# Moving where the split weights begin in their tiles: 52 bytes instead of 64

## The chip, the cores and the metric

The kernel runs on one core of a Trainium2 chip. The metric is the device time of one execution in microseconds; the shown number is the median of three executions.

## The reference, cut to what matters

Two transformer blocks run one after the other on 256 tokens of width 1024. The first has a gated feed-forward layer (width 2816), a mixer with two kinds of attention and gates, and a second gated feed-forward layer. The second has a mixer of a convolution and a retention, a cross attention to 256 memory rows, and a feed-forward layer of width 4096 with a squared ReLU. Everything is float32. Nearly all the work is in products of activations with weight matrices that are read once:

```python
def swiglu(h, w_in, w_out):
    gu = h @ w_in
    gate, up = jnp.split(gu, 2, axis=-1)
    return (jax.nn.silu(gate) * up) @ w_out
...
def sq_relu_mlp(h, up_w, down_w):
    return jnp.square(jax.nn.relu(h @ up_w)) @ down_w
```

## The kernel before, in words

**Layout.** Activations lie feature by token: 128 features of a block on the partitions, the tokens along the free dimension (272 tokens up to the first attention, because of 16 meta tokens; 256 from there on). A weight block of 128 by 128 is the stationary operand of a matmul and the activations are the moving operand. `_plan` (L43) writes down the order in which all weight blocks are used and packs them into chunks of up to 2048 columns.

**Three products for one.** Each factor is split into a high part in the chip's reduced float32 format (fp32r) and a low part, the rest. `mm3` (L512) makes three matmuls for each weight block: high weight by high activation (L513), high weight by low activation (L514), low weight by high activation (L515). Each of them loads its weight block anew. Counting the loops of the program there are 2,360 blocks that go this way, so 7,080 such matmuls, and 144 more in `products_t` (L995), where the weight part is the moving operand (512 columns, L1005 to L1007) and the activation is loaded.

**The split of the weights.** `_Weights` brings a chunk into a tile `raw` by DMA (`load`, L291), ScalarE writes the high part (`_high`, L319) and VectorE the low part (`piece`, L335). `piece` is called between the other work in `_Core.step`, so that the parts are ready ahead of their use. The tiles `hi` and `lo` come from `_part`, three of each: a tile is 64 columns (`LINE`) wider than the chunk, and the part begins `SHIFT` columns behind the tile's start:

```python
        t = self.pool.tile([P, CH + LINE], F32R, tag=tag, bufs=3, name=f"{tag}{c}")
        return t[:, SHIFT : SHIFT + CH]
```

**Where operands begin.** The tiles that serve as moving operands of `mm3` (`XH`, `XL`, `AH`, `AL`, `YH`, `YL`, `MH`, `ML`, `CH`, `CL` and the like) and their rows per block are multiples of 64 columns, that is of 256 bytes, and so are the `hi` and `lo` tiles. All of them therefore begin at one place modulo 256 bytes. A weight block has 128 columns (512 bytes), so each block begins as many bytes behind that place as the whole part does: 64 with `SHIFT` 16. Some matmuls take their moving operand in two pieces of 128 columns, the second 576 bytes behind the first (`qv`, L498); the call is `xq`. In one product (`fa`) the weight blocks are only 8 columns wide, so that successive blocks begin 32 bytes apart.

**Other matmuls.** Scores, transposes, statistics (`rms`, L559, matmul L562) and head norms (L766) run in plain float32; they break the stream of the fp32r matmuls at the borders of the layers and all through the attention.

Of the kernel before, what the change touches and what calls it, by code (L numbers as in the profile page):

```python
# [23 lines left out]
TP = 288  # L24
XP = 320
LINE = 64
SHIFT = 16
DFF = 2816
MF = DFF // P
DFF2 = 4096  # L30
# [244 lines left out]
class _Weights:  # L275
# [30 lines left out]
    def _part(self, tag, c):  # L306


        t = self.pool.tile([P, CH + LINE], F32R, tag=tag, bufs=3, name=f"{tag}{c}")
        return t[:, SHIFT : SHIFT + CH]  # L310

# [1294 lines left out]
```

## Time and profile before

| what | value |
|---|---|
| median of 3 executions | 982.52 us |
| lowest, highest | 981.97, 982.52 us |
| the profiled execution's own time | 983.64 us |
| its span, first to last instruction | 981.6 us |
| mean granted TensorE clock | 0.998 |
| TensorE: matmuls, busy share | 7,667, 98% |
| VectorE, ScalarE busy share | 69%, 55% |

The profile is of one execution. Of its 983.64 us, 981.6 lie between the first and the last instruction and some 2 around them. A matmul's record runs from its start until its result is out, so the records of successive matmuls overlap; the time that one takes from the next is the distance of their starts. A window of the profile counts each matmul that it touches, also the two or three that only overlap its edges.

### The profile page before, as it was taken

The numbers are of one execution on the slowest core, as the hardware profiler recorded it, in microseconds if no ns is written. First come the engines' busy times: TensorE is split into PE (matmuls) and PEld (weight loads), VectorE is DVE, ScalarE is ACT, GpSimd is POOL, SyncE is SP. The second block draws the span as 40 slices with busy tenths as digits, with TensorE's granted clock in tenths as the row PEclk, the third lists the DMA queues.
The fourth block names the chain that finished last, engine by engine and source line by source line (L and its number), as shares of the span: only waits on it lengthen the run. The fifth ranks groups of instructions, "written<-read, shape, count | busy, mean of one in ns | idle before, by whom it ended". The sixth has DMA issues, their size and how long they took to land.

```text
span 981.6 us, 18397 instructions
## 1 busy us (share of the span) xinstructions
PE 965.1 (98%) x7667; PEld 935.2 (95%) x7667; DVE 675.4 (69%) x1232; ACT 537.5 (55%) x927; POOL 9.9 (1%) x15
## 2 busy tenths in 40 slices
PE   7999999999999999999999999999999999999996
PEld 7999999999989899999999999889899999999996
DVE  5686656657875758677666657999976677675552
ACT  6545444456574656666454447556484566554441
POOL 0000000020000000000000000000000000000000
PEclk9999999999999999999999999999999999999999
DMA  8674526554523225554544656443544256555431
GB/s 298 191 264 172 173 92 233 191 185 138 173 94 123 96 99 214 215 215 173 194 166 157 209 191 235 168 155 138 202 159 155 86 182 221 199 194 194 173 128 43
DMA packets 31363, 169.05 MB, mean 172 GB/s; under 512 B 5144, under 2 KB 8864, under 8 KB 14640
## 3 DMA queue, kind: packets, MB, share of 16 engines
q1 hardware_dynamic: 30928, 167.34, 48.3%
q8 instruction: 60, 0.98, 0.4%
q10 hardware_dynamic: 288, 0.52, 0.1%
q14 instruction: 23, 0.19, 0.1%
q0 software_dynamic: 64, 0.01, 0.0%
HBM read 166.79 MB, written 1.07 MB: 171 GB/s over the span
## 4 chain that ended last, share of the span: by engine, by line
PE 75%; ACT 1%; DVE 1%; issue 0%; DVEq 0%
PE ps L513 14%; PE ps L515 14%; PE ps L514 14%; PE po L515 7%; PE po L514 7%; PE po L513 7%; PE ps L660 1%; PE ps L1007 1%; PE ps L1006 1%; PE ps L1005 1%; PE po L702 1%; PE ps L1308 1%; PE ps L1174 0%; PE po L1346 0%; PE po L716 0%; PE ps L766 0%
## 5 line engine op out<-in xcount | busy, mean ns | idle before, releaser
L335 DVE TENSOR_TENSOR lo<-raw,hi 128x1024 fp32r<-128x1024 f32 (+2 forms) x334 | 373.4, 1130 | 47.5 <-ACT hi L319 45.0
L319 ACT ACTIVATE hi<-raw 128x1024 fp32r<-128x1024 f32 (+2 forms) x334 | 321.8, 978 | 137.2 <-issue 43.8
L513 PE MATMUL ps<-XH,hi 128*128 128x256 f32 (+2 forms) x976 | 284.0, 291 | 5.7 <-ACT hi L319 4.3
L515 PE MATMUL ps<-XH,lo 128*128 128x256 f32 (+2 forms) x976 | 277.4, 284 | 0.8 <-DVE lo L335 0.8
L514 PE MATMUL ps<-XL,hi 128*128 128x256 f32 (+2 forms) x976 | 277.6, 284 | 0.0
L513 PEld LDWEIGHTS ps<-XH,hi 128*128 128x128 f32 (+1 forms) x976 | 184.4, 189 | 8.2 <-ACT hi L319 4.3
L514 PEld LDWEIGHTS ps<-XL,hi 128*128 128x128 f32 (+1 forms) x976 | 186.0, 191 | 1.8 <-DVE XL L527 0.5
L515 PEld LDWEIGHTS ps<-XH,lo 128*128 128x128 f32 (+1 forms) x976 | 184.3, 189 | 1.4 <-DVE lo L335 1.0
L513 PE MATMUL po<-XH,hi 128*128 128x256 f32 (+1 forms) x456 | 130.2, 285 | 0.2 <-DVE br L1071 0.2
L515 PE MATMUL po<-XH,lo 128*128 128x256 f32 (+1 forms) x456 | 129.0, 283 | 0.4 <-DVE lo L335 0.4
L514 PE MATMUL po<-XL,hi 128*128 128x256 f32 (+1 forms) x456 | 128.7, 282 | 0.0
L514 PEld LDWEIGHTS po<-XL,hi 128*128 128x128 f32 x456 | 86.7, 190 | 0.1
L515 PEld LDWEIGHTS po<-XH,lo 128*128 128x128 f32 x456 | 85.8, 188 | 0.6 <-DVE lo L335 0.6
L513 PEld LDWEIGHTS po<-XH,hi 128*128 128x128 f32 x456 | 85.7, 188 | 0.6 <-DVE br L1071 0.5
L624 ACT ACTIVATE s<-gr 128x272 f32<-128x272 f32 (+1 forms) x44 | 18.7, 426 | 108.5 <-DVE gr L622 108.5
L513 PE MATMUL ps<-AHf,hi 128*128 128x272 f32 (+1 forms) x220 | 62.4, 284 | 0.0
L514 PE MATMUL ps<-ALf,hi 128*128 128x272 f32 (+1 forms) x220 | 62.4, 284 | 0.0
L515 PE MATMUL ps<-AHf,lo 128*128 128x272 f32 (+1 forms) x220 | 62.4, 284 | 0.0
L1045 DVE SCALAR_TENSOR_TENSOR cv<-U,par,cv 128x256 f32<-128x256 f32 x120 | 50.1, 479 | 0.2 <-ACT cv L1078 0.2
L622 DVE TENSOR_TENSOR gr<-ps,r 128x272 f32<-128x272 f32 (+1 forms) x28 | 12.1, 434 | 48.4 <-PE ps L515 42.1
L513 PE MATMUL ps<-AHm,hi 128*128 128x256 f32 x160 | 45.0, 281 | 0.0
L514 PE MATMUL ps<-ALm,hi 128*128 128x256 f32 x160 | 45.0, 281 | 0.0
(385 smaller groups left out, 1827.8 us busy)
## 6 DMA issues: line engine op xcount, KB each, us to landing
raw<-in_ws_dram SPq DMA_DIRECT2D x128, 1024.0 KB, 4.8
raw<-in_ws_dram SPq DMA_DIRECT2D x32, 704.0 KB, 4.2
raw<-in_ws_dram SPq DMA_DIRECT2D x3, 512.0 KB, 5.6
dec<-in_dec_dram SPq DMA_DIRECT2D x1, 1536.0 KB, 6.4
BM<-drow SPq DMA_DIRECT2D x2, 512.0 KB, 5.7
memraw<-in_mt_dram SPq DMA_DIRECT2D x1, 1024.0 KB, 7.0
hA<-in_xt_dram SPq DMA_DIRECT2D x3, 273.0 KB, 6.0
raw<-in_ws_dram SPq DMA_DIRECT2D x3, 256.0 KB, 6.7
```

Source lines behind the costliest of these rows:

```text
L319: self.nc.scalar.activation(self.hi[c][:, a:b], self.raw[c][:, a:b], AF.Copy)
L335: self.nc.vector.tensor_tensor(self.lo[c][:, a:b], self.raw[c][:, a:b], self.hi[c][:, a:b].bitcast(F32), op=ALU.subtract)
L513: T.matmul(o, w[0], x[0], start=start, stop=False)
L514: T.matmul(o, w[0], x[1], start=False, stop=False)
L515: T.matmul(o, w[1], x[0], start=False, stop=stop)
L622: V.tensor_tensor(gr, g[:, :n], r[0][:, :n], op=ALU.mult)
L624: S.activation(s, gr, AF.Silu)
L660: T.matmul(ps[:, at : at + n], lhs, rhs, start=True, stop=True)
L702: T.matmul(o, st["v"](h, 0), pt[:, :SEQ], start=t % 2 == 0, stop=False)
L1005: T.matmul(ps[i], xh[:, t], wh, start=k == 0, stop=False)
L1006: T.matmul(ps[i], xl[:, t], wh, start=False, stop=False)
L1045: V.scalar_tensor_tensor(cv[:, m], U[:, m, j : j + SEQ], prm("cw", m * 31 + j), cv[:, m], op0=ALU.mult, op1=ALU.add)
```

## The change

`SHIFT` goes from 16 to 13. Both parts of each weight chunk then begin 52 bytes behind the place where the moving operands begin, and so does every weight block of 128 columns. The tiles stay where they are and keep their size; no instruction, wait or DMA is added or removed. ScalarE and VectorE write the parts 12 bytes earlier, TensorE loads its weights 12 bytes earlier (in `products_t` it streams them from 12 bytes earlier), and 52 is no multiple of 16.

```diff
 LINE = 64
-SHIFT = 16
+SHIFT = 13
 DFF = 2816
```

## Rows read from the trace of the kernel before

**Rows 1.** Clock and span of the core, then TensorE's busy line of the page
```profile
core 0: 981.6 us, clock 0.998
...
PE 965.1 (98%) x7667; PEld 935.2 (95%) x7667; DVE 675.4 (69%) x1232; ACT 537.5 (55%) x927; POOL 9.9 (1%) x15
```

**Rows 2.** Waits of TensorE's matmuls: engine, line, waited for, us, times, longest
```profile
PE ps L513 <- ACT hi L319: 4.3, 1, 4.3
PE ps L513 <- ACT XH L521: 1.4, 1, 1.4
```

**Rows 3.** Windows, TensorE alone: stretch, its length, busy (matmuls), clock, DMA
```profile
30.93:211.13 180.20, 180.20 (x1462) 1.00 0.54 183
...
356.80:410.86 54.06, 54.06 (x479) 1.00 0.55 199
411.53:589.61 178.08, 178.08 (x1515) 1.00 0.53 184
600.98:614.02 13.04, 13.04 (x117) 1.00 0.37 123
...
720.80:738.14 17.34, 17.34 (x155) 1.00 0.52 182
774.01:799.40 25.39, 25.39 (x227) 1.00 0.49 172
800.06:972.37 172.31, 172.31 (x1465) 1.00 0.45 164
...
590.92:598.69 7.77, 7.77 (x68) 1.00 1.00 406
667.93:681.94 14.01, 14.01 (x121) 1.00 0.32 122
738.81:744.34 5.53, 5.53 (x49) 1.00 0.53 190
```

**Rows 4.** The chain that ended last, three of its pieces: start us, us, what
```profile
411.14 0.43 PE ps L562 x2
...
598.86 0.45 PE ps L562 x2
...
799.67 0.43 PE ps L562 x2
```

**Rows 5.** Timeline of matmuls whose moving operand is in two pieces (256 columns)
```profile
235.80 0.28 PE L514 MATMUL po<-XL,hi 128*128 128x256 f32 x1
...
236.40 0.28 PE L513 MATMUL po<-XH,hi 128*128 128x256 f32 x1
```

**Rows 6.** Timeline of the product with weight blocks of 8 columns
```profile
237.32 0.29 PE L514 MATMUL ps<-XL,hi 128*8 128x272 f32 x1
...
239.93 0.28 PE L514 MATMUL ps<-XL,hi 128*8 128x272 f32 x1
```

**Rows 7.** Groups of weight loads by shape: busy us, mean ns
```profile
L514 PEld LDWEIGHTS ps<-XL,hi 128*128 128x128 f32 x968 | 185.3, 191 | 1.4 <-DVE XL L527 0.5
...
L514 PEld LDWEIGHTS ps<-XL,hi 128*8 128x8 f32 x8 | 0.7, 89 | 0.4
```

**Rows 8.** Weight loads of L690 in 270:311, then 312:350: ns min/median/max, first and last
```profile
L690 PEld LDWEIGHTS ps<-cst,p x8: 138/139/144, 271.5 to 305.6; 128*128 128x128 f32 x8
...
L690 PEld LDWEIGHTS ps<-cst,p x8: 138/141/143, 313.4 to 348.9; 128*128 128x128 f32 x8
```

**Rows 9.** Timeline of two plain float32 transposes of 128 columns
```profile
271.39 0.27 PE L688 MATMUL ps<-cst,p 128*128 128x128 f32 x1
271.50 0.27 PE L689 MATMUL ps<-cst,p 128*128 128x128 f32 x1
```

**Rows 10.** VectorE and ScalarE: the split's groups by shape, then L1045's durations min/median/max
```profile
L335 DVE TENSOR_TENSOR lo<-raw,hi 128x1024 fp32r<-128x1024 f32 x291 | 352.6, 1219 | 47.2 <-ACT hi L319 44.7
...
L319 ACT ACTIVATE hi<-raw 128x1024 fp32r<-128x1024 f32 x291 | 303.0, 1050 | 132.7 <-issue 43.8 <-PE ps L514 36.7 <-PE po L514 29.0
...
L1045 DVE SCALAR_TENSOR_TENSOR cv<-U,par,cv x120: 470/479/489, 608.6 to 705.5; 128x256 f32<-128x256 f32 x120
```

## The prediction

> **What bounds the kernel now.** I read the clock and the busy line first, then TensorE's waits, then windows over single stretches, then the timeline. The clock was granted in full, the 2.4 GHz level, and TensorE is busy for 98% of the span [rows 1]. Its matmuls hardly ever wait for another engine: the longest wait is 4.3 us, once, at the start [rows 2]. So the time is the sum of the distances from one matmul start to the next, and the reader should turn the windows into such distances. Two matmuls are taken off each window's count for those that only overlap its edges. The window 356.80 to 410.86 gives 54.06 us / 477 = 113.3 ns for a matmul with 256 moving columns; the next one, 411.53 to 589.61, gives 178.08 / 1,513 = 117.7 ns for the same form [rows 3]. 600.98 to 614.02, 720.80 to 738.14 and 774.01 to 799.40 again show 113.3, 113.3 and 112.8; 800.06 to 972.37 shows 117.8, and so do three short windows with 66, 119 and 47 matmuls [rows 3]. Between a cheap and a dear stretch stands a break of the stream, such as the statistics matmul of L562: 113.3 ns before the one at 411.14 and 117.7 behind it, 117.8 before 598.86 and 113.3 behind 600.98, 113 before 799.67 and 117.8 behind it to the end [rows 3, 4]. The operands begin at the same places modulo 256 on both sides. So the stream has two paces, falls into one of them at a break, and keeps it for up to 1,513 matmuls. With 272 columns there is one pace in the long window, 180.20 / 1,460 = 123.4 ns [rows 3]; with the moving operand in two pieces it is (236.40 - 235.80) / 5 = 120 ns [rows 5].
>
> **The change part by part.** No instruction, wait or DMA comes or goes, and no tile moves.
>
> The writes of the parts: ScalarE's take 1,050 ns and VectorE's 1,219 ns for 1,024 columns [rows 10]. L1045 reads its input at every multiple of 4 bytes, 120 times, and takes 470 to 489 ns throughout [rows 10]; so a start off 16 bytes costs VectorE nothing that I can see there. For ScalarE I take the same by that nearest row; if it lost 19 ns a piece (the spread of L1045), that is 291 x 19 ns = 5.5 us, spread over an engine busy for 55%, with TensorE not waiting for it. Cover: both engines run ahead of the products. Price 0; without the cover at most 5.5 us.
>
> The loads of the weights: L690 loads 128 columns from 576 bytes behind a tile's start in the first window and from 580 in the second, where the block begins 4 bytes behind a multiple of 16. The medians are 139 and 141 ns [rows 8]. So such a load costs 0 to 2 ns. These are plain float32 loads, the only ones of this kind in the trace. A load of 8 columns takes 89 ns against 191 for 128 [rows 7], or 0.85 ns a column; but with the short load matmuls of 272 columns still start 2.61 us / 21 = 124.3 ns apart [rows 6], against 123.4 with the full load. The length of the load therefore doesn't set the pace, and I take 0 of these 2 ns, keeping 2 for the range.
>
> The place of the load against the moving stream: this is what is left, and where the effect must lie if there is one. A moving column costs at most 113.3 / 256 = 0.44 ns, a loaded one 0.85 ns, so the moving stream gains 1.1 columns per ns on the load that runs beside it. It makes up a lead of 16 columns in some 14.6 ns and one of 13 in 11.8 (estimates from these rows). The change thus lets every meeting of the two streams come 2.7 ns earlier, while the two paces lie 4.4 ns apart. It takes no meeting away. No row has a load that begins 52 bytes behind, beside an fp32r matmul, so the price of a matmul with 256 columns must be bounded: from above by 120 ns, the dearest steady pace of that width [rows 5]; from below by 110 ns, the distance of two plain transposes with full loads [rows 9]. I take 113.3, the cheap pace, for all stretches. The reason is weak and I say so: that pace is steady under the old place too, and 3,208 matmuls in the windows run at the dear one against 970 at the cheap one, so a new draw has more to win than to lose. For 272 columns, for two pieces and for `products_t` I take no change.
>
> The sum: the dear windows hold 1,513 + 1,463 + 66 + 119 + 47 = 3,208 matmuls; at 4.4 ns each that is 14.1 us. The profiled execution took 983.64 us, of which 981.6 is the span; 983.64 - 14.1 = 969.5. The median of the three runs is 1.1 lower, 982.52; so the median after should be **968 us**, 1.4% less.
>
> Two pages bear on this, and nothing above hangs on them. By the Trainium skill, page "TensorE: Matmul & The Clock Gate", section "Step-by-step: what each phase is for", the moving operand and the weight load have read ports of their own, and loading the next weights takes no read bandwidth from the running matmul. By that rule the place of the load would be of no account and the time would stay at 982.5 (rival 1); two paces for one form speak against it, without refuting it. By its page "SBUF — State Buffer", section "Specifications (TRN2)", memory is read in lines of 16 bytes and each new line costs something; a load from 52 bytes touches 33 lines instead of 32. By that rule the kernel would get slower (rival 2); the 2 ns of the loads agree with it.
>
> **The rivals.**
> 1. Nothing happens: each stretch keeps its pace and the time stays at 982.5 us. For it: the paces change with no change of place. Against it: something finer than the place modulo 256 decides, and 2.7 ns is of the size of the difference.
> 2. Slower by the crooked start: the 2 ns of the load pass into the pace of the matmuls. It decides as soon as the next matmul waits for the end of its load. 7,080 x 2 ns = 14.2 us, so 996.7 us. An irregular meeting like that of the two pieces gives the same: 970 x 6.7 ns + 3,208 x 2.3 ns = 13.9 us. Against it: the pace with the short loads [rows 6].
> 3. Slower by the dear pace: all stretches fall into it. 970 x 4.4 ns = 4.3 us more, 986.8 us. For it: it is the commoner one.
> 4. Only one of the two long stretches changes: 14.1 / 2 = 7 us less, 975.5 us.
> 5. A pace below both, 110 ns: 3,208 x 7.7 + 970 x 3.3 ns = 27.9 us less, 954.6 us; lower still if the 272 columns follow. Against it: no fp32r stretch shows it.
>
> **How the numbers follow.** The forecast has 0.35, rivals 1 to 5 have 0.14, 0.18, 0.13, 0.10 and 0.10. What a measurement here can tell from no change is about 0.2%, 2 us. Faster is the forecast with rivals 4 and 5, 0.55; the same is rival 1, 0.14; slower is rivals 2 and 3, 0.31. Both signs hold much, so the range reaches from rival 5, with some of the 272 columns, to rival 2: 949 to 997 us. The forecast's own range is 964 to 973.
>
> **What would show it.** Right: windows of 256 columns all at 113.3 ns, no dear stretch behind L562, 123.4 for 272 columns, durations of L319 and L335 within some ns of 1,050 and 1,219. The prediction is wrong if the dear pace stands in the long stretches, if a third pace appears, if the 272 columns move, or if the loads behind fp32r matmuls lengthen and the pace with them. A clock below 1.00 or a TensorE that waits for `hi` or `lo` would mean that the writes of the parts count after all.

## The result and the profile after

The changed kernel takes 971.62 us in the median of four executions (970.48 to 974.0), against 982.52 us before. The ratio is 0.9891, 95% interval 0.9879 to 0.9904: 1.1% faster, 968 us was forecast. The profiled execution took 971.08 us, 12.6 us less than that of before.

The clock, then TensorE's busy line of the page, which answer to [rows 1]; then its longest waits, which answer to [rows 2]:

```profile
core 0: 969.1 us, clock 0.998
```

```profile
PE 953.0 (98%) x7667; PEld 922.5 (95%) x7667; DVE 673.9 (70%) x1232; ACT 538.3 (56%) x927; POOL 9.9 (1%) x15
```

```profile
PE ps L513 <- ACT hi L319: 4.3, 1, 4.3
PE ps L513 <- ACT XH L521: 1.3, 2, 1.1
```

TensorE makes as many matmuls, waits as little and is busy for the same share; the clock is the same too. The time has gone out of the distances between the matmuls. Windows of TensorE of the changed kernel (columns as in [rows 3]):

```profile
30.16:213.59 183.43, 183.43 (x1462) 1.00 0.53 180
358.21:411.59 53.38, 53.38 (x474) 1.00 0.55 201
412.37:524.79 112.42, 112.42 (x994) 1.00 0.49 175
525.37:583.74 58.37, 58.37 (x517) 1.00 0.66 221
794.10:959.68 165.58, 165.58 (x1463) 1.00 0.47 171
608.96:611.60 2.64, 2.64 (x23) 1.00 0.43 137
641.18:643.82 2.64, 2.64 (x24) 1.00 0.36 149
```

Two matmuls come off each count again. The stretches that ran at 117.7 and 117.8 ns before, from 411 to 590 and from 800 to 972, now run at 112.42 / 992 = 113.3, 58.37 / 515 = 113.3 and 165.58 / 1,461 = 113.3 ns; the one that was cheap before is unchanged (53.38 / 472 = 113.1). The stretch from 412 to 584 is shown in two windows, because one distance at 525 took 0.22 us. With 272 columns the long window has become dearer: 183.43 / 1,460 = 125.6 ns, against 123.4. And a new pace of about 120 ns stands in some stretches of one product each, between the plain float32 matmuls of the second mixer: 2.64 us for 22 matmuls, the last two windows (the first of them touches one neighbour only).

The matmuls whose moving operand is in two pieces, answering to [rows 5], in the timeline:

```profile
226.71 0.28 PE L513 MATMUL ps<-XH,hi 128*128 128x256 f32 x1
...
227.88 0.28 PE L514 MATMUL ps<-XL,hi 128*128 128x256 f32 x1
```

Ten distances in 1.17 us, 117 ns instead of 120. The writers of the parts, answering to [rows 10]:

```profile
L335 DVE TENSOR_TENSOR lo<-raw,hi 128x1024 fp32r<-128x1024 f32 x291 | 353.3, 1222 | 46.4 <-ACT hi L319 44.4
...
L319 ACT ACTIVATE hi<-raw 128x1024 fp32r<-128x1024 f32 x291 | 304.3, 1055 | 128.4 <-issue 43.2 <-PE ps L514 35.6 <-PE po L514 25.6
```

3 and 5 ns more for 1,024 columns: nothing that TensorE waits for. The loads of the weights, answering to [rows 7], have not become longer, 189 ns against 191:

```profile
L514 PEld LDWEIGHTS ps<-XL,hi 128*128 128x128 f32 x968 | 183.3, 189 | 1.4 <-DVE XL L527 0.5
```

The balance of the largest terms: 2,976 matmuls in the two long stretches at 4.4 ns less, 13.1 us; 119 + 47 of the short ones, which are cheap now too, 0.7 us; 576 matmuls in two pieces (24 products of 8 blocks) at 3 ns less, 1.7 us; and 183.43 - 180.20 = 3.2 us more in the long window of 272 columns. 13.1 + 0.7 + 1.7 - 3.2 = 12.3, and 12.6 were measured. The stretches of single products went both ways. The three short stretches in the windows of the changed kernel:

```profile
584.81:592.94 8.13, 8.13 (x71) 1.00 1.00 407
662.56:676.05 13.49, 13.49 (x121) 1.00 0.32 122
732.88:738.21 5.33, 5.33 (x49) 1.00 0.54 195
```

13.49 / 119 and 5.33 / 47 give 113.4 ns; the first stayed dear, 8.13 / 69 = 117.8. In front of it TensorE waits 0.57 us for a low part, and up to that wait the stream runs at 113.3 ns; so a wait inside a stretch can change the pace too.

### The profile page after: what moved, and what is told of

It is laid out like the page before. It is cut to its first block, busy times and chain, and to the rows that moved or that the text cites. A ratio compares the mean times of both kernels' runs of the same rounds, so it can differ in the third digit from the quotient of the medians.

```text
span 969.1 us, 18397 instructions
## 1 busy us (share of the span) xinstructions
PE 953.0 (98%) x7667; PEld 922.5 (95%) x7667; DVE 673.9 (70%) x1232; ACT 538.3 (56%) x927; POOL 9.9 (1%) x15
## 4 chain that ended last, share of the span: by engine, by line
PE 96%; ACT 1%; DVE 1%; DMA 1%; SPq 0%; issue 0%; DVEq 0%
PE ps L513 19%; PE ps L514 18%; PE ps L515 18%; PE po L514 10%; PE po L515 10%; PE po L513 10%; PE ps L660 1%; PE ps L1007 1%; PE ps L1005 1%; PE ps L1006 1%; PE po L702 1%; DMA raw<-in_ws_dram 1%; PE ps L1308 1%; PE ps L1174 0%; PE po L716 0%; PE po L1346 0%
## 5 line engine op out<-in xcount | busy, mean ns | idle before, releaser
L514 PEld LDWEIGHTS ps<-XL,hi 128*128 128x128 f32 (+1 forms) x976 | 184.0, 189 | 1.8 <-DVE XL L527 0.5
L1045 DVE SCALAR_TENSOR_TENSOR cv<-U,par,cv 128x256 f32<-128x256 f32 x120 | 50.2, 481 | 0.2 <-ACT cv L1078 0.2
L515 PE MATMUL ps<-AHm,lo 128*128 128x256 f32 x160 | 44.2, 276 | 0.0
```

Source lines behind the costliest of these rows:

```text
L514: T.matmul(o, w[0], x[1], start=False, stop=False)
L515: T.matmul(o, w[1], x[0], start=False, stop=stop)
L1045: V.scalar_tensor_tensor(cv[:, m], U[:, m, j : j + SEQ], prm("cw", m * 31 + j), cv[:, m], op0=ALU.mult, op1=ALU.add)
```

## The experiments

Theory after the result: the distance in bytes between the start of a weight block and the start of the moving operand beside it decides between a few steady paces, and at 52 bytes the cheap one lasts. Rivals: the start off a multiple of 16 bytes does it (whatever the distance); or the stretches merely drew the cheap pace in this build. All paces are means over the matmuls of a window. Runs 1 to 11 were single executions with a profile; the kernel before took 982.82 us beside the first eight and 982.67 (median of seven) beside the rest.

**Moving the activations instead of the weights.** Runs 1 and 2 give the tiles `XH` and `XL` 64 more columns and begin them some columns in; all other moving operands stay.

```diff
-    XH = base.tile([P, KD, XP], F32R, name="XH")
+    XH = base.tile([P, KD * XP + LINE], F32R, name="XH")[:, 61 : 61 + KD * XP].rearrange("p (k n) -> p k n", n=XP)
```

Run 1, 61 columns (12 bytes back, modulo 256) with `SHIFT` 13:

> SHIFT 13, but the activations XH and XL begin 12 bytes earlier too (modulo 256), so that the weights lie 64 bytes behind them again while they begin off 16 bytes, and still 52 behind all other moving operands. If the distance of the load from the moving operand sets the pace: the XH stretches of 256 columns go back to two paces (117.8 ns in most), the stretches of the other operands (AHf, AHm, YH, OXH) stay at 113.3 ns, and the time is 976 to 982 us. If the start off 16 bytes does it: 113.3 ns everywhere, 971 us.

Run 2, 3 columns (12 bytes on) with `SHIFT` 16:

> SHIFT 16 as before, but XH and XL begin 12 bytes later, so that the weights, on multiples of 16 bytes, lie 52 bytes behind them, and 64 behind all other moving operands. If the distance sets the pace: the XH stretches of 256 columns run at 113.3 ns and their 272 columns at 125.6, the stretches of AHf and AHm at 113.3 or 117.8 as a break leaves them; 972 to 980 us. If the start of the weights off 16 bytes does it: XH as before, 117.8 ns in most, 982 us.

Run 1 took 993.35 us, run 2 988.38. Windows of TensorE of run 1: 256 columns of XH, of AHf, of XH, of AHm, then 272 columns of XH and of AHf.

```profile
419.94:535.38 115.44, 115.44 (x965) 1.00 0.47 168
540.03:595.12 55.09, 55.09 (x489) 1.00 0.65 221
811.61:895.37 83.76, 83.76 (x700) 1.00 0.52 184
895.72:982.09 86.37, 86.37 (x765) 1.00 0.40 144
30.91:149.46 118.55, 118.55 (x914) 1.00 0.51 172
149.46:214.58 65.12, 65.12 (x530) 1.00 0.58 193
```

XH runs at 115.44 / 963 = 119.9 and 83.76 / 698 = 120.0 ns, AHf and AHm at 113.1 and 113.2. At 895.0 the stream passes from XH to AHm with no other matmul between, and within a microsecond the pace has fallen. So the place of the moving operand counts as well as that of the load, and the start of the weights off 16 bytes alone is not what helps: XH has the same weights. But XH did not go back to the two old paces; moved off 16 bytes itself, it takes a dearer one (distances of 117 and 123 ns in turn), also with 272 columns (118.55 / 912 = 130.0 ns). AHf with 272 columns ran at 65.12 / 528 = 123.3 ns here, with the same places as in the changed kernel, where it had 125.6. Run 2, windows of XH:

```profile
414.51:590.47 175.96, 175.96 (x1497) 1.00 0.53 181
804.75:977.07 172.32, 172.32 (x1466) 1.00 0.46 163
```

Each window holds products of XH first, 52 bytes apart, and then of AHf or AHm, 64 apart; both run at one pace, 117.7 ns. (Elsewhere in this run, from 403 to 413, XH ran at 116.7 ns.) The distance alone does not give the cheap pace.

**Other places of the weights.** Only `SHIFT` is changed, for run 4 also the tiles' width (`CH + 2 * LINE`). Run 3, 48 bytes:

> SHIFT 12, 48 bytes, a multiple of 16. If the distance sets the pace and small steps count little: 113.3 ns for 256 columns and 970 to 976 us. If the start off 16 bytes is what helps: 117.8 ns in the long stretches, about 982 us.

Run 4, 308 bytes:

> SHIFT 77, 52 + 256 bytes, in tiles that are 64 columns wider. If only the place modulo 256 counts: the paces of the changed kernel, 113.3 ns for 256 columns and 125.6 for 272, and 971 to 972 us. If each build draws its paces anew at the breaks: other paces in some stretches, anywhere from 965 to 987 us.

Run 5, 68 bytes:

> SHIFT 17, 68 bytes: 4 behind a multiple of 16, as 52 is, but one multiple further on. If the column within the 16 bytes sets the pace: 113.3 ns for 256 columns everywhere and about 971 us. If it is the distance of 52 from the moving operand: dear stretches again, 982 to 993 us.

Run 6, 116 bytes:

> SHIFT 29, 116 bytes, 52 + 64. If the column within 16 bytes, or the place within 64, sets the pace: 113.3 ns for 256 columns, about 971 us. If only the place within 256 does: other paces, 975 to 995 us.

Run 7, 56 bytes:

> SHIFT 14, 56 bytes: one column further than the change, two columns behind a multiple of 16. If any start off 16 bytes gives the cheap pace: 113.3 ns for 256 columns and about 971 us. If it takes the one column of 52 bytes: 117.8 ns or dearer in the long stretches, 980 us or more.

Windows of TensorE with 256 columns, one fence for each of runs 3, 5, 6 and 7:

```profile
809.43:981.73 172.30, 172.30 (x1465) 1.00 0.46 162
```

```profile
807.11:980.23 173.12, 173.12 (x1465) 1.00 0.46 161
```

```profile
813.26:987.19 173.93, 173.93 (x1463) 1.00 0.45 160
```

```profile
820.00:970.00 150.00, 150.00 (x1275) 1.00 0.48 169
```

| bytes behind | time, us | ns for 256 columns, last layer | ns for 272 columns, long window |
|---|---|---|---|
| 48 | 993.02 | 172.30 / 1,463 = 117.8 | 126.7 |
| 52 | 971.62 | 113.3 | 125.6 (123.3 in run 11) |
| 56 | 987.22 | 150.00 / 1,273 = 117.8 | 123.3 |
| 64 | 982.52 | 117.8 (113.3 in other stretches) | 123.4 |
| 68 | 991.50 | 173.12 / 1,463 = 118.3 | 124.1 |
| 116 | 998.48 | 173.93 / 1,461 = 119.0 | 126.8 |

Run 4 took 972.32 us: 52 + 256 bytes do what 52 do, and in another build. The same two long stretches run at the cheap pace, 112.40 / 992 = 113.3 and 165.50 / 1,460 = 113.4 ns, so that the rival of the chance of one build falls for them:

```profile
413.60:526.00 112.40, 112.40 (x994) 1.00 0.50 175
795.40:960.90 165.50, 165.50 (x1462) 1.00 0.48 170
```

Of the six places within 256 bytes only 52 gives the cheap pace in all long stretches (run 12 below has an exception); 4 bytes more or less lose it in every stretch, also where 64 had it. 68 and 116 bytes begin 4 bytes behind a multiple of 16, as 52 does, and are dear, so that the rival of the crooked start falls. 48 and 64 begin on a multiple of 16 and 56 does not, and 56 lies between them: a start on 16 bytes neither helps nor hurts by itself. 116 is 52 + 64: the place counts within more than 64 bytes.

**The high parts alone.** Run 8:

```diff
-        return t[:, SHIFT : SHIFT + CH]
+        at = 13 if tag == "hi" else SHIFT
+        return t[:, at : at + CH]
```

> The high parts alone begin 52 bytes behind, the low parts stay at 64. Two of three loads are of high parts. If each load's own start sets what its neighbours wait: a pace of 256 columns between the two, about a third of the gain lost, 974 to 977 us. If the whole stream falls into one pace: all at 113.3 ns (971 us) or the long stretches at 117.8 (982 us).

986.59 us. Windows of TensorE: 272 columns, then three stretches of 256.

```profile
30.91:214.35 183.44, 183.44 (x1462) 1.00 0.54 180
360.12:413.17 53.05, 53.05 (x470) 1.00 0.56 203
413.71:591.79 178.08, 178.08 (x1514) 1.00 0.53 184
803.01:975.32 172.31, 172.31 (x1465) 1.00 0.46 164
```

The two long stretches run at 117.8 ns and the one before them at 113.4, as before the change; the 272 columns run at 125.6. Two loads of three at 52 bytes bring none of the gain and the full loss with 272 columns. Only the mean is the old one: in the last layer the distance behind a block's first, second and third matmul is 120.0, 117.6 and 115.8 ns by the starts in the trace, where the kernel before has 117.6, 118.3 and 117.4. Runs 1, 2, 3, 6 and 8 all took longer than any time that was expected for them.

**The distance again, on multiples of 16.** Run 9 begins XH and XL 16 bytes on (4 columns) and has `SHIFT` 17, so that nothing but the weights begins off 16 bytes:

> SHIFT 17 (68 bytes, 118.3 ns everywhere in the run before) with XH and XL moved on by 16 bytes: the weights lie 52 bytes behind XH and XL, which begin on a multiple of 16, and 68 behind all other moving operands. If the distance to the moving operand sets the pace: XH stretches of 256 columns at 113.3 ns and of 272 at 125.6, two pieces at 117.0, AHf and AHm still at 118.3; about 981 us. If the place of the load itself counts: XH too at 118.3, 991 us.

992.32 us. Windows of TensorE: 256 columns of XH, of AHf:

```profile
403.50:525.50 122.00, 122.00 (x1027) 1.00 0.51 182
525.94:591.15 65.21, 65.21 (x553) 1.00 0.58 196
```

XH runs at 122.00 / 1,025 = 119.0 ns, not at 113.3; AHf at 65.21 / 551 = 118.3, as in run 5. My theory of the distance falls with that: load and moving operand lie as in the changed kernel, both 16 bytes further on, and the pace is another.

**Breaks.** Runs 10 and 11 put seven plain float32 matmuls of the statistics' kind into the last layer, whose results nobody reads, into the kernel before and into the changed one:

```diff
+            def cut():
+                ps = bank()
+                T.matmul(ps[:, :SEQ], k0("ones"), acc_in[:, :SEQ], start=True, stop=True)
...
+                if m in (7, 12, 18, 24):
+                    cut()
...
+                if m in (1, 3, 5):
+                    cut()
```

> The kernel before with seven more plain float32 matmuls of the statistics' kind, whose results nobody reads, in the last layer, which runs at 117.8 ns throughout. If the pace is drawn at a break and kept to the next: some of the stretches between them run at 113.3 ns, others at 117.8. If the place in memory or the kind of layer sets it: 117.8 in all of them. Each break itself costs about 0.6 us, so 983 to 987 us in all.

> The changed kernel with the same seven matmuls. If 52 bytes leave only one pace that lasts: every stretch between the breaks returns to 113.3 ns, and the time is 971.6 plus some 4 us for the breaks. If the changed kernel only happened to fall into the cheap pace: dear stretches appear among them.

Run 10 took 983.97 us. The windows between its breaks:

```profile
800.11:814.12 14.01, 14.01 (x121) 1.00 0.39 137
815.15:828.07 12.92, 12.92 (x117) 1.00 0.58 217
828.73:845.58 16.85, 16.85 (x146) 1.00 0.55 190
846.60:862.24 15.64, 15.64 (x140) 1.00 0.51 172
862.90:905.19 42.29, 42.29 (x362) 1.00 0.56 197
906.22:927.29 21.07, 21.07 (x188) 1.00 0.52 179
927.96:950.46 22.50, 22.50 (x194) 1.00 0.48 174
951.48:972.56 21.08, 21.08 (x188) 1.00 0.00 1
```

The reader is to divide again: 117.7, 112.3, 117.0, 113.3, 117.5, 113.3, 117.2 and 113.3 ns. (Where a window cuts into a neighbour, three are to be taken off instead of two, which moves a value by up to 1 ns.) Dear and cheap alternate at every one of these breaks, and between them the pace holds: the stretch that was dear up to a break is cheap behind it. Other interruptions don't keep to this. In the middle of another stretch TensorE waits 0.4 us for a low part; the kernel before runs at 117.7 ns on both sides of that wait (the windows from 411.53 and from 590.92 in [rows 3]), while run 10, with the same instructions up to there, goes from 117.8 to 6.68 / 59 = 113.2 ns:

```profile
590.16 0.39 PE L515 MATMUL po<-XH,lo 128*128 128x256 f32 x1 [0.44 <-DVE lo L335]
```

```profile
591.31:597.99 6.68, 6.68 (x61) 1.00 0.99 401
```

The seven breaks cost so little in all because half of the layer got cheaper. Run 11 took 971.75 us; its stretches in the same layer:

```profile
791.70:804.96 13.26, 13.26 (x119) 1.00 0.38 133
805.74:819.00 13.26, 13.26 (x119) 1.00 0.61 229
819.78:835.76 15.98, 15.98 (x143) 1.00 0.57 201
...
938.94:960.36 21.42, 21.42 (x191) 1.00 0.00 1
```

13.26 / 117 = 113.3, 113.3, 113.3 and 21.42 / 189 = 113.3 ns, and the four others like them. In this layer 52 bytes return to the cheap pace behind every break. They do not do so everywhere: behind the statistics at 591 the next stretch of this run has 13.92 / 116 = 120.0 ns, where the changed kernel has 12.47 / 110 = 113.4. The first window is of run 11, the second of the changed kernel:

```profile
592.11:606.03 13.92, 13.92 (x118) 1.00 0.38 131
```

```profile
595.81:608.28 12.47, 12.47 (x112) 1.00 0.40 128
```

The 272 columns ran at 123.3 ns in this execution (180.21 us in the long window), not at 125.6.

**Two places.** Run 12 gives 64 bytes to the chunks whose products have 272 columns and 52 to the rest; it was executed four times:

```diff
-        return t[:, SHIFT : SHIFT + CH]
+        first = next(k for k, _, _, _, _ in self.chunks[c])[0]
+        at = SHIFT_T1 if first in T1_TAGS else SHIFT
+        return t[:, at : at + CH]
```

with `SHIFT_T1 = 16` and `T1_TAGS = ("f1g", "d1", "ka", "fa", "va")`.

> 64 bytes for the chunks whose products have 272 columns (first feed-forward layer, keys, forget gate and values of the first attention), 52 for all others. If each stretch's pace depends only on its own distance: 123.3 ns for 272 columns and 113.3 for 256, so 971.6 less some 1,700 x 2.2 ns = 3.7 us, about 968 us. If the chunks affect each other: the 256 columns show dear stretches again, 972 us or more.

969.05 us in the median of four (968.1 to 972.09), ratio 0.9859 to the kernel before, 0.9842 to 0.9875; this beats both kernels, the changed one by some 0.3%, as far as two ratios from different measurements can be set side by side. The profiled execution is its slowest, 972.09 us. Its windows:

```profile
30.12:210.31 180.19, 180.19 (x1462) 1.00 0.55 183
408.91:521.34 112.43, 112.43 (x995) 1.00 0.50 175
521.68:583.72 62.04, 62.04 (x518) 1.00 0.63 210
795.09:960.78 165.69, 165.69 (x1464) 1.00 0.48 170
```

123.4 ns for 272 columns, as meant, and 113.2 and 113.3 for 256; but one long stretch, the down products of the second feed-forward layer, ran at 62.04 / 516 = 120.2 ns, where the changed kernel had 113.3 with the same places. That is 516 x 6.9 = 3.6 us, about what this execution has over the other three; whether they had 113.3 there no profile shows. The dear pace begins at 521.7, behind a single distance of 0.22 us; the changed kernel has the same one at 525 and keeps 113.3. So at 52 bytes too a dear pace can last.

## Why the prediction was right

**The bound.** Right: nothing but the distances of the starts moved. Clock, waits and busy share are as before.

**The writes.** Price 0 was right; ScalarE's 5 ns and VectorE's 3 ns for a piece are covered. ScalarE's don't come from the crooked start: at 48 bytes, a multiple of 16, its writes took 1,055 ns too (run 3).

**The loads off 16 bytes.** Right that they don't matter by their start: 68 bytes cost as much as 48, and the loads took 189 ns instead of 191. So rival 2 is out. What the Trainium skill says on the page "SBUF — State Buffer", section "Specifications (TRN2)", of a penalty for each new line of 16 bytes does not order the six places: the fastest of them is off the lines and its neighbour on the line is dear.

**The cheap pace in all long stretches.** Right in the size, 13.8 of the 14.1 us, and in the mechanism as far as it went: of two steady paces the cheap one holds in the long stretches. Rival 1 is out: four bytes either way change the time by 1.6 and 2.2%. The separate read ports that the Trainium skill's page "TensorE: Matmul & The Clock Gate", section "Step-by-step: what each phase is for", tells of can't be taken to mean that the place is of no account. Rivals 3, 4 and 5 did not come.

**The reason given for it was weak and does not explain it.** I took the new place for a new draw. In the last layer run 10 shows no draw at 64 bytes but an alternation from break to break, and run 11 that at 52 the cheap pace comes back each time. Elsewhere it does look like a draw: the same wait left the pace at 117.7 ns in the kernel before and changed it in run 10, and at 52 bytes runs 11 and 12 have 120 ns in stretches where the changed kernel has 113.3. With 48, 56, 68 and 116 bytes the same wager would have lost: one place of five tried beside the old one wins. The forecast was right by luck in that respect; a chance of 0.35 was generous by what these runs show.

**No change for 272 columns and for the pieces.** Wrong in size: +3.2 us in the profiled execution and -1.7 us. Two of the signs by which the prediction was to be known as wrong did come: the 272 columns moved, and a third pace of 120 ns stands in stretches of one product. They cost too little to undo the gain. The terms of the 272 columns and of the pieces are most of what separates the measured 12.6 us from the 14.1. With 272 columns 52 bytes have two paces themselves, 125.6 in the profiled execution and in run 4, 123.3 in run 11; in run 1 AHf had 123.3. The 3.5 us between the fastest and the slowest execution of the changed kernel are of the size of that difference (1,460 x 2.2 ns = 3.2 us), but it can't be the only cause: the profiled execution, which had the dear one, took 971.08 us, 0.6 more than the fastest. A long stretch at 120 ns, as in run 12, would cost about as much. Which of them the other executions had no profile shows.

**What stays open.** What makes the paces. It is not the distance of load and moving operand alone (runs 2 and 9), nor the column within 16 bytes (runs 5 and 6), nor either operand alone (run 1: XH and AHm share the weights; runs 3 to 7: they share the moving operands); both places count, since a change of either alone changes the pace. Nor does a dear pace need the writers of the parts or the DMA to go on: at the end of the kernel before, when both have ended, 12.87 us still hold matmuls at 12.87 / 109 = 118 ns. The window gives TensorE's matmuls and loads, VectorE, ScalarE and GpSimd, then clock, DMA share and GB/s:

```profile
959.50:972.37 12.87, 12.87 (x111) 12.87 (x110) 1.28 (x3) 0.93 (x2) 0.00 (x0) 1.00 0.00 1
```

Whether writers or DMA take part when a pace is set, and what sets it, no run here tells.

## What to carry to other kernels

Where TensorE is the bound, divide windows by their matmuls: a steady distance that differs between stretches of one form is time to be had, which busy shares don't show. Try the start of the stationary operand in steps of one column, not of 16, with the moving operands at one place modulo 256, and measure each; the best place has to be looked for by width of the moving operand. A single profile shows one choice of pace, so time several executions.

## What the runs showed of the hardware

At a granted clock of 1.00 the mean distance of fp32r matmuls with 256 columns took a few values here, 113.3, 116.7, 117.8, 118.3, 119.0 and 120 ns, kept for up to 1,513 matmuls. The single distances below a mean can differ, 120.0, 117.6 and 115.8 ns in run 8. With the weights 64 bytes behind, a plain float32 matmul in the last layer flipped the mean between 113.3 and 117.8, eight stretches in turn (run 10); a wait inside a stretch changed it in one execution and not in another. Without any break it followed the moving operand's place within a microsecond (run 1, 120.0 to 113.2 ns). Eight full loads from 4 bytes behind a multiple of 16 took a median of 141 ns [rows 8] in the kernel before and 138 in the changed one, where nothing about them differs; so the 2 ns of the prediction lie within the scatter.
